# Low halves of woven weights: made by an adding DMA in place of GpSimd's subtraction, and used last

## The chip, the core and the metric

The kernel runs on one core of a Trainium2 chip. The metric is the device time of one execution in microseconds (us), lower is better. Engines: TensorE (PE, with its weight loads PEld), VectorE (DVE), ScalarE (ACT), GpSimd (POOL) and SyncE (SP, which issues nearly all DMAs).

## The reference

One layer of a hybrid model over 640 tokens: 128 of a prompt and 512 of a 2-D grid, with 1024 features. Everything is float32.

```python
def _trunk_layer(x, cvec, s0, ctx_k, ctx_v, p):
    sh1, sc1, g1, sh2, sc2, g2 = _modulation(cvec, p["w_ada"], p["b_ada"])
    h = _rmsnorm(x, p["norm1_g"]) * (1.0 + sc1) + sh1
    u_rw, u_na, gate_rw, gate_na = jnp.split(h @ p["w_in"], IN_SPLITS, axis=-1)
    o_rw, s_new = _rwkv_branch(u_rw, s0, ...)      # recurrent scans, forward and backward
    ...
    o_na = _na_latent(q, k, v, ctx_k, ctx_v, p["na_rpb"])   # or _na_context for the prompt
    merged = (jax.nn.sigmoid(gate_rw) * (o_rw @ p["w_o_rwkv"])
              + jax.nn.sigmoid(gate_na) * (o_na @ p["w_o_na"]))
    x = x + g1 * (merged @ p["w_out"])
    h2 = _rmsnorm(x, p["norm2_g"]) * (1.0 + sc2) + sh2
    x = x + g2 * ((jax.nn.silu(h2 @ p["ffn_w1"]) * (h2 @ p["ffn_w3"])) @ p["ffn_w2"])
    return x, s_new, k, v
```

## The kernel before, in words

**Split products.** A float32 matrix is written as the sum of a rounded matrix (`hi`, type float32r) and the remainder (`lo`). A product is three matmuls: hi weights by hi input, hi weights by lo input, lo weights by hi input. `feat_gen` (L188) yields these one at a time for one half of the tokens (320 of 640) and one chunk of 128 output features: 8 tiles of 128 input features by 3 products are 24 matmuls, two halves 48.

**Weight chunks.** `wdma` (L157) has SyncE load a chunk (128x1024 float32, 512 KB) into a staging tile `wst`, of which there are two in this stage. `wcast` (L166) has ScalarE copy it into `whi`, which rounds it (L170). Then VectorE or GpSimd writes `wlo` = `wst` - `whi` (L175); GpSimd does so in pieces of 256 columns. The next load into the same buffer starts when that subtraction has read it.

**Units.** Between about 120 and 690 us of the span the kernel works off 47 units (`stream`, L740) in an order written out by hand: `k`, `r`, `v`, `l` (projections of the recurrent branch), `g` (gates), then the merges `a0` to `a7` (neighbourhood output, 4 input tiles, chunks of 128x512, 24 matmuls) and `b0` to `b7` (recurrent output, 3 input tiles, 128x384, 18 matmuls; the order is `b2`, `b4`, `b3`, `b5`). A string with one letter for each unit says which engine makes its low half: VectorE for the first nine and `a4`, GpSimd (`p`) for the other 37: 22 chunks of 128x1024, 7 of 128x512 and 8 of 128x384. Units `k1` to `b7` are GpSimd's.

**The weave.** From about 254 us on, the units fill TensorE's time between the parts of the recurrent scan, in four passes over pairs of heads. Each pass has `main`, `inv` (inversion of triangular blocks on VectorE: `pr` at L1249 and `RL` at L1253, ending in `f`, L1262), `carry` (a chain that goes back and forth between TensorE and ScalarE, L1323, L1326, L1350) and `out` (L1411). `AG` (L1104) and `ZV` (L1375) are VectorE's inputs to such products. A table sets how many matmuls of a unit go between two steps. A unit's cast is issued an eighth of the way into the unit before it. Inside the weave the orders of TensorE, GpSimd, VectorE and ScalarE are those of the code; SyncE's queue, and the other engines after the weave, go by the scheduler's simulated times.

**Merges and the end.** Before `a0`, twelve loads (`o_load`, L1435) fetch the neighbourhood output's hi and lo parts (`o_d_80`, `o_d_81`) into two tiles `o`, which take the places of `h` (hi, lo). A merge unit multiplies `o`, and VectorE adds the gate (`mt`, L1463). After `b7` comes a product over the last input tile with one more chunk of `w_o` (L1575), whose sums are multiplied with gate parts `pre` and `tr` (loads at L1569), and then the product with `w_out`, added to the residual `x`.

Of the kernel before, what the change touches and what calls it, by code (L numbers as in the profile page):

```python
# [7 lines left out]
F32 = mybir.dt.float32  # L8
F32R = mybir.dt.float32r
AF = mybir.ActivationFunctionType  # L10
ALU = mybir.AluOpType
# [90 lines left out]
def V(ap, dims, off=0):  # L102

    return bass.AP(ap.tensor, ap.offset + off, [list(ap.ap[0])] + [list(d) for d in dims])
# [3 lines left out]
def body(ctx: ExitStack, tc: tile.TileContext, xs, xp, cols, consts, w_ada, b_row, w_rw, w_qkv,  # L108
# [3 lines left out]
    pe, act, dve, pool, sp = nc.tensor, nc.scalar, nc.vector, nc.gpsimd, nc.sync  # L112
# [22 lines left out]
    def nm(s):  # L135
        cn[0] += 1
        return f"{s}_{cn[0]}"
# [28 lines left out]
    def wcast(w, eng=None):  # L166
        st, n, pl, nhl = w
        hi = pl.tile([P, 1024], F32R, tag="whi", bufs=nhl, name=nm("whi"))
        lo = pl.tile([P, 1024], F32R, tag="wlo", bufs=nhl, name=nm("wlo"))
        act.copy(hi[:, :n], st[:, :n])  # L170
        eng = eng or dve
        step = 256 if eng is pool else n
        for a in range(0, n, step):
            b = min(a + step, n)
            eng.tensor_tensor(out=lo[:, a:b], in0=st[:, a:b], in1=hi[:, a:b].bitcast(F32), op=ALU.subtract)  # L175
        return hi, lo

    def wload(src, eng=None):
        return wcast(wdma(src), eng)
# [8 lines left out]
    def feat_gen(ps, chunk, act_hl, nk, t0, t1, width=128, wcol=0, k0=0):  # L188

        hi, lo = chunk  # L190
        xh, xl = act_hl
        n = 0
        for kt in range(nk):
            a = kt * width + wcol
            for (w, x) in ((hi, xh), (hi, xl), (lo, xh)):
                pe.matmul(ps[:, :t1 - t0], w[:, a:a + 128], x[:, k0 + kt, t0:t1],  # L196
                          start=n == 0, stop=n == 3 * nk - 1)
                n += 1
                yield

    def drain(g):
        for _ in g:
# [2 lines left out]
    def feat_mm(*args, **kw):  # L205
        for _ in feat_gen(*args, **kw):
            pass
# [295 lines left out]
    def proj_gen(ci, out, ps_, usb, utag, ubufs, w):  # L503
        U = usb.tile([P, 643], F32, tag=utag, bufs=ubufs, name=nm("U"))
        pool.memset(V(U[:, :], [[513, 2]]), 0.0)
        pool.memset(U[:, 642:643], 0.0)
        ps0 = ps_()
        yield from feat_gen(ps0, w, (hh, hl), 8, 0, H2)
        later(lambda: act.copy(U[:, 1:321], ps0[:, :H2]))
        ps1 = ps_()  # L510
        yield from feat_gen(ps1, w, (hh, hl), 8, H2, NT)

        def u_out():
            act.copy(U[:, 321:513], ps1[:, 0:192])
            act.copy(U[:, 514:642], ps1[:, 192:320])

        def shift(a, b, u):
            o = out[:, a:b]
            n = b - a
            act.activation(o, U[:, u:u + n], AF.Identity, scale=dcol(dm, ci))  # L520
            dve.scalar_tensor_tensor(out=o, in0=U[:, u - 1:u - 1 + n], scalar=col("mu0", ci),
                                     in1=o, op0=ALU.mult, op1=ALU.add)
            dve.scalar_tensor_tensor(out=o, in0=U[:, u + 1:u + 1 + n], scalar=col("mu1", ci),
                                     in1=o, op0=ALU.mult, op1=ALU.add)

        later(u_out, (0.6, 0))
        later(lambda: shift(512, 640, 514), (0.4, 0.7), 2)
        later(lambda: shift(0, 512, 1), (0.8, 1.5), 5)
# [190 lines left out]
    def unit(g, e):  # L719

        i, eng = int(g[1:]), eng_of(e)
        if g[0] in "ab":
            return 24 if g[0] == "a" else 18, lambda: merge_load(g[0], i), \
                lambda wt: merge_cast(*wt, eng), lambda w: merge_gen(g[0], i, w)
        if g[0] == "g":
            return 48, lambda: wdma(w_rw[15 + i]), lambda w: wcast(w, eng), \
                lambda w: gate_gen(i, w, flps, sb, gtag[-1])
        ci, dst = {"k": (4 + i, kt_), "r": (i, rt_), "v": (8 + i, vp0), "l": (12 + i, lg_)}[g[0]]
        return 48, lambda: wdma(w_rw[ci]), lambda w: wcast(w, eng), \
            lambda w: proj_gen(ci, dst, flps, sb, "U", len(gtag), w) if g[0] != "l" else lora_gen(i, w)  # L730
# [48 lines left out]
    with s1:  # L779
# [25 lines left out]
        with s1a:  # L805
            for b, dst, gcol in ((0, qT, dcol(dqg)), (1, kT, col("kg"))):
# [10 lines left out]
                for i in range(5):  # L817
# [10 lines left out]
                                      in0=V(qr[:, :], [[64, 8], [1, 64]]),  # L828
                                      in1=V(r[:, :], [[1, 8], [0, 64]]), op=ALU.mult)
                    if b == 1 and i == 4:  # L830
                        kout = tb.tile([P, 512], F32, tag="vt", bufs=2, name="kout")
                        dve.tensor_tensor(out=V(kout[:, :], [[64, 8], [1, 64]]),
                                          in0=V(qn[:, :], [[64, 8], [1, 64]]),
                                          in1=V(kgb[:, :], [[0, 8], [1, 64]]), op=ALU.mult)
# [4 lines left out]
                    for f in range(4):  # L839
                        src = pst[:, f * 128:(f + 1) * 128]  # L840
                        if i < 4:
                            out = V(dst[f], [[1, 2], [8, 64]], 2 * i)
                            src = V(src, [[64, 2], [1, 64]])
                        else:
                            out = dst[f][:, 512:640]
# [27 lines left out]
        with ExitStack() as s1b:  # L873
# [127 lines left out]
            with tc.manual_schedule(engines=FIRST):  # L1001
                for k, step in enumerate(PRM["na"].split()):
                    a, p, b, q, n = (int(x) for x in step.split("."))
# [994 lines left out]
```

## Time and profile before

| | |
|---|---|
| time, median of 3 runs | 1202.04 us (1201.33 to 1202.62) |
| profiled execution | 1203.88 us, of which the span is 1202.1 us |
| mean granted TensorE clock | 0.975 |
| busy: TensorE, weight loads, VectorE, ScalarE, GpSimd | 94%, 84%, 67%, 42%, 23% |
| GpSimd's subtractions (L175) | 118 pieces, 100.7 us |

A profile row with "x4" joins four instructions in a row; where a bracket ends the row, it gives the idle time of the engine ahead of it and what ended that. A row of waits gives the waiting engine and line, the engine and line that released it, the total in us, how often, and the longest. All times within an execution count from the start of the span.

### The profile page before, as it was taken

What the parts mean: (1) busy time and instruction counts of PE and PEld (TensorE: products, weight loads), DVE (VectorE), ACT (ScalarE), POOL (GpSimd) and SP (SyncE); (2) the same over time, 40 slices, a digit from 0 to 9 for tenths busy, and PEclk for the clock granted to TensorE, in tenths of its full rate; (3) what the DMA queues carried; (4) which work ended last, traced back from release to release, by engine and by line L of the source; (5) the groups of instructions that cost most, each with busy time, mean ns of one, the idle gap of its engine ahead of it and who ended that gap; (6) DMA issues with size and microseconds to landing.
All of it is one profiled execution on the core that took longest, in us unless ns stands there. A gap on an engine that the chain in (4) does not pass through costs nothing.

```text
span 1202.1 us, 26930 instructions
## 1 busy us (share of the span) xinstructions
PE 1134.1 (94%) x11160; PEld 1006.9 (84%) x11160; DVE 799.6 (67%) x1630; ACT 503.6 (42%) x1016; POOL 271.8 (23%) x354
## 2 busy tenths in 40 slices
PE   6999999999899899999879999989999999999998
PEld 4688877788888888888778878889889989998997
DVE  4565555569659848946584584888568756875675
ACT  4444655553454564355322331754224422442240
POOL 1162244343224324332221360200001000000000
PEclk8999999999899999999889989999999999999999
DMA  9762767531211221120442571312312231222222
GB/s 335 251 122 83 245 207 231 190 123 49 66 48 37 89 63 54 66 70 30 167 131 75 178 271 58 106 36 88 106 53 88 89 103 56 88 89 88 69 72 104
DMA packets 56578, 134.48 MB, mean 112 GB/s; under 512 B 7140, under 2 KB 22116, under 8 KB 56456
## 3 DMA queue, kind: packets, MB, share of 16 engines
q1 hardware_dynamic: 55592, 131.56, 33.6%
q8 instruction: 88, 1.44, 0.5%
q10 hardware_dynamic: 864, 1.20, 0.3%
q14 instruction: 34, 0.28, 0.1%
HBM read 118.41 MB, written 14.32 MB: 110 GB/s over the span
## 4 chain that ended last, share of the span: by engine, by line
PE 58%; DVE 15%; DMA 2%; ACT 2%; issue 2%; SPq 0%; POOL 0%; DVEq 0%; ACTq 0%
PE f L1717 21%; PE acc L283 16%; PE fl L196 10%; DVE pr L1249 2%; DVE RL L1253 2%; PE w L1363 1%; PE w L1323 1%; PE w L1350 1%; DVE AG L1156 1%; PE w L1335 1%; PE mm L196 1%; DVE TG L1159 1%; DVE Rt L1283 1%; DVE AG L1104 1%; DMA tr<-trw_d 1%
## 5 line engine op out<-in xcount | busy, mean ns | idle before, releaser
L196 PE MATMUL fl<-h,whi 128*128 128x320 f32 x704 | 169.7, 322 | 0.0
L175 POOL TENSOR_TENSOR wlo<-wst,whi 128x256 fp32r<-128x256 f32 x118 | 100.7, 882 | 203.2 <-ACT whi L170 199.8
L1717 PE MATMUL f<-t,whi 128*128 128x320 f32 x640 | 141.4, 309 | 0.0
L1717 PE MATMUL f<-b,whi 128*128 128x320 f32 x608 | 136.4, 312 | 3.6 <-ACT b L185 1.8
L283 PE MATMUL acc<-whi,u 128*128 128x512 f32 (+1 forms) x448 | 136.1, 385 | 0.0
L196 PEld LDWEIGHTS fl<-h,whi 128*128 128x128 f32 x704 | 120.6, 191 | 4.5 <-issue 0.2
L170 ACT CAST whi<-wst 128x1024 fp32r<-128x1024 f32 (+2 forms) x86 | 81.9, 957 | 79.3 <-PE acc L283 28.3
L196 PE MATMUL fl<-h,wlo 128*128 128x320 f32 x352 | 114.1, 324 | 0.0
L1717 PEld LDWEIGHTS f<-t,whi 128*128 128x128 f32 x640 | 107.0, 188 | 0.0
L1717 PEld LDWEIGHTS f<-b,whi 128*128 128x128 f32 x608 | 102.8, 190 | 4.8 <-ACT b L185 2.2
L1772 POOL TENSOR_TENSOR ws<-wst 128x512 f32<-128x512 f32 x20 | 27.8, 1390 | 341.6 <-DVE wlo L1761 226.7
L1717 PE MATMUL f<-t,wlo 128*128 128x320 f32 x320 | 98.9, 309 | 0.0
L283 PEld LDWEIGHTS acc<-whi,u 128*128 128x128 f32 x448 | 83.5, 188 | 16.7
L1717 PE MATMUL f<-b,wlo 128*128 128x320 f32 x304 | 94.7, 311 | 1.4 <-DVE wlo L1761 1.4
L1758 ACT CAST whi<-ws 128x1024 fp32r<-128x1024 f32 x40 | 42.0, 1050 | 108.7 <-PE f L1717 48.4
L283 PE MATMUL acc<-wlo,u 128*128 128x512 f32 (+1 forms) x224 | 86.3, 385 | 0.0
L175 DVE TENSOR_TENSOR wlo<-wst,whi 128x1024 fp32r<-128x1024 f32 (+1 forms) x49 | 60.6, 1243 | 35.3 <-ACT whi L170 34.8
L283 PE MATMUL acc<-whi,h 128*128 128x512 f32 x240 | 79.3, 404 | 0.2 <-DVE h L397 0.2
L196 PE MATMUL fl<-o,whi 128*128 128x320 f32 x224 | 58.9, 342 | 13.7 <-DVE mt L1463 5.7
L196 PEld LDWEIGHTS fl<-h,wlo 128*128 128x128 f32 x352 | 67.4, 192 | 2.6 <-issue 0.2
L1557 DVE SCALAR_TENSOR_TENSOR tt<-acc,G 128x512 f32<-128x512 f32 (+1 forms) x51 | 34.7, 680 | 50.7 <-PE acc L283 50.7
L196 PE MATMUL mm<-h,whi 128*128 128x320 f32 x288 | 67.8, 323 | 0.0
(332 smaller groups left out, 2587.6 us busy)
## 6 DMA issues: line engine op xcount, KB each, us to landing
wst<-in_w_dram SPq DMA_DIRECT2D x66, 512.0 KB
wst<-in_w_rw_dram SPq DMA_DIRECT2D x31, 512.0 KB
wa<-in_w_ada_dram SPq DMA_DIRECT2D x24, 512.0 KB
f<-in_w_ada_dram SPq DMA_DIRECT2D x16, 512.0 KB
wst<-in_w_qkv_dram SPq DMA_DIRECT2D x12, 512.0 KB
o<-o_d SPq DMA_DIRECT2D x14, 320.0 KB
x<-in_xs_dram SPq DMA_DIRECT2D x8, 512.0 KB
wa<-in_w_ada_dram SPq DMA_DIRECT2D x16, 256.0 KB
```

The source lines that it names most:

```text
L170: act.copy(hi[:, :n], st[:, :n])
L175: eng.tensor_tensor(out=lo[:, a:b], in0=st[:, a:b], in1=hi[:, a:b].bitcast(F32), op=ALU.subtract)
L196: pe.matmul(ps[:, :t1 - t0], w[:, a:a + 128], x[:, k0 + kt, t0:t1], start=n == 0, stop=n == 3 * nk - 1)
L283: pe.matmul(pss[i][:, a:b], lhs(x, kt, ts_), w[:, cs_], start=ki == 0 and n == 0, stop=ki == last and n == 2)
L1104: dve.tensor_tensor(out=AG[rr, c, h, :], in0=c64(S.kk[rr, :], d), in1=S.P65[d][rr, :, 0:64], op=ALU.mult)
L1156: dve.tensor_tensor(out=AG[oth, ls, h, :], in0=sq(pg, n)[oth], in1=V(K[oth, :], [[0, n], [1, 64]], KO["strict"]), op=ALU.mult)
L1249: dve.tensor_tensor(out=prv, in0=V(RL[:, s + 1 + a, :], [[32, b - a], [0, s]], s), in1=V(RL[:, s, :], [[0, b - a], [1, s]]), op=ALU.mult)
L1253: dve.tensor_tensor(out=dst, in0=dst, in1=prv, op=ALU.add)
L1557: dve.scalar_tensor_tensor(out=tt, in0=ps[:, a:b], scalar=c, in1=G[:, g, sl], op0=ALU.mult, op1=ALU.mult)
L1717: pe.matmul(ps[:, :H2], w_[:, c_], x_[:, kt, :], start=first and kt + n == 0, stop=last and kt == 3 and n == 2, skip_group_check=more)
L1758: act.copy(r[0][:, :width], src())
L1772: eng_x(PRM["se"][i - 1]).tensor_tensor(out=o_, in0=x, in1=y, op=op)
```

## The change

For a unit of GpSimd, ScalarE first writes the negated chunk, rounded, to `wlo`; then GpSimd issues one DMA that adds the staged chunk to `wlo` (`accum_op`), and ScalarE makes `whi` as before. The sum is `wst` minus the rounded `wst`, the same low half. VectorE's units keep their subtraction. In `feat_gen` the order of a half's matmuls is new for all units: all products with hi weights come first, then all with low weights.

```diff
@@ -167,12 +167,12 @@
         st, n, pl, nhl = w
         hi = pl.tile([P, 1024], F32R, tag="whi", bufs=nhl, name=nm("whi"))
         lo = pl.tile([P, 1024], F32R, tag="wlo", bufs=nhl, name=nm("wlo"))
+        if eng is pool:
+            act.activation(lo[:, :n], st[:, :n], AF.Copy, scale=-1.0)
+            pool.dma_start(lo[:, :n].bitcast(F32), st[:, :n], accum_op=ALU.add)
         act.copy(hi[:, :n], st[:, :n])
-        eng = eng or dve
-        step = 256 if eng is pool else n
-        for a in range(0, n, step):
-            b = min(a + step, n)
-            eng.tensor_tensor(out=lo[:, a:b], in0=st[:, a:b], in1=hi[:, a:b].bitcast(F32), op=ALU.subtract)
+        if eng is not pool:
+            dve.tensor_tensor(out=lo[:, :n], in0=st[:, :n], in1=hi[:, :n].bitcast(F32), op=ALU.subtract)
         return hi, lo
 
     def wload(src, eng=None):
@@ -190,13 +190,14 @@
         hi, lo = chunk
         xh, xl = act_hl
         n = 0
-        for kt in range(nk):
-            a = kt * width + wcol
-            for (w, x) in ((hi, xh), (hi, xl), (lo, xh)):
-                pe.matmul(ps[:, :t1 - t0], w[:, a:a + 128], x[:, k0 + kt, t0:t1],
-                          start=n == 0, stop=n == 3 * nk - 1)
-                n += 1
-                yield
+        for ps_ in (((hi, xh), (hi, xl)), ((lo, xh),)):
+            for kt in range(nk):
+                a = kt * width + wcol
+                for (w, x) in ps_:
+                    pe.matmul(ps[:, :t1 - t0], w[:, a:a + 128], x[:, k0 + kt, t0:t1],
+                              start=n == 0, stop=n == 3 * nk - 1)
+                    n += 1
+                    yield
 
     def drain(g):
         for _ in g:
```

Lines behind L170 move by one. ScalarE's queue at the first two GpSimd units (`wlo_2813` is `k1`'s; `U` and `on` are other work), before:

```order
L542 ACTIVATE U_2746<-mm_2747 128x320
L170 COPY whi_2812<-wst_2671 128x1024
L185 COPY on_2535<-po_2822 128x128
L542 ACTIVATE U_2801<-mm_2802 128x320
L170 COPY whi_2912<-wst_2799 128x1024
L542 ACTIVATE U_2845<-mm_2846 128x320
```

and with the change:

```order
L543 ACTIVATE U_2746<-mm_2747 128x320
L171 ACTIVATE wlo_2813<-wst_2671 128x1024
L173 COPY whi_2812<-wst_2671 128x1024
L185 COPY on_2535<-po_2820 128x128
L543 ACTIVATE U_2801<-mm_2802 128x320
L543 ACTIVATE U_2843<-mm_2844 128x320
L171 ACTIVATE wlo_2911<-wst_2799 128x1024
```

The negated copy (L171) stands right ahead of each cast, and nothing else is put between; the second unit's cast moves one place back among the `U` rows.

GpSimd's queue at the same place, before:

```order
L921 TENSOR_TENSOR L_2709<-L_2709,m_2710 128x128
L175 TENSOR_TENSOR wlo_2813<-wst_2671,whi_2812 128x256 x4
L1496 MEMSET Nt 128x1280
L505 MEMSET U_2901 128x2
L506 MEMSET U_2901 128x1
L175 TENSOR_TENSOR wlo_2913<-wst_2799,whi_2912 128x256 x4
L1203 MEMSET ZV 64x2x64 x2
```

and with the change:

```order
L922 TENSOR_TENSOR L_2709<-L_2709,m_2710 128x128
L172 DMA wlo_2813<-wst_2671 128x1024
L1497 MEMSET Nt 128x1280
L506 MEMSET U_2899 128x2
L507 MEMSET U_2899 128x1
L172 DMA wlo_2911<-wst_2799 128x1024
L1204 MEMSET ZV 64x2x64 x2
```

Each group of four subtractions becomes one DMA issue at the same place in the queue.

SyncE's queue at the loads of `o` ahead of the merges (`o_d_80` hi, `o_d_81` lo; `tna_d` is a store of gate parts), before:

```order
L543 DMA tna_d<-fl_7589 128x320
L1435 DMA o_7754<-o_d_81 128x640 x2
L1435 DMA o_7753<-o_d_80 128x640 x3
L1435 DMA o_7754<-o_d_81 128x640
L1435 DMA o_7753<-o_d_80 128x640
L1435 DMA o_7754<-o_d_81 128x640
L1435 DMA o_7753<-o_d_80 128x640
L1435 DMA o_7754<-o_d_81 128x640
L1435 DMA o_7753<-o_d_80 128x640
L1435 DMA o_7754<-o_d_81 128x640
L543 DMA tna_d<-fl_7640 128x320
```

and with the change:

```order
L163 DMA wst_7723<-in_w_o_dram 128x512
L544 DMA tna_d<-fl_7545 128x320
L1436 DMA o_7710<-o_d_81 128x640 x6
L1436 DMA o_7709<-o_d_80 128x640 x6
L544 DMA tna_d<-fl_7596 128x320
L163 DMA wst_7942<-in_w_o_dram 128x512
```

The loads of the two parts, which alternated from the third on, now come as six of the low part and then six of the high part.

SyncE's queue at the end of the merges, before:

```order
L1449 DMA mx_9051<-trw_d 128x640
L1569 DMA pre_9175<-trw_d 128x640
L163 DMA wst_9155<-in_w_out_dram 128x1024
L163 DMA wst_9527<-in_w_out_dram 128x1024
L163 DMA wst_9575<-in_w_out_dram 128x1024
L1547 DMA x_0_9131<-in_xs_dram 128x1024
L1547 DMA x_1_9132<-in_xs_dram 128x1024
L1547 DMA x_2_9133<-in_xs_dram 128x1024
L1547 DMA x_3_9134<-in_xs_dram 128x1024
L1547 DMA x_4_9135<-in_xp_dram 128x1024
L1569 DMA tr_9177<-trw_d 128x640
L1569 DMA tr_9179<-trw_d 128x640
```

and with the change:

```order
L163 DMA wst_9105<-in_w_o_dram 128x8x128
L1570 DMA pre_9131<-trw_d 128x640
L163 DMA wst_9111<-in_w_out_dram 128x1024
L163 DMA wst_9483<-in_w_out_dram 128x1024
L1548 DMA x_0_9087<-in_xs_dram 128x1024
L1548 DMA x_1_9088<-in_xs_dram 128x1024
L1548 DMA x_2_9089<-in_xs_dram 128x1024
L1548 DMA x_3_9090<-in_xs_dram 128x1024
L1548 DMA x_4_9091<-in_xp_dram 128x1024
L1570 DMA tr_9133<-trw_d 128x640
L1570 DMA tr_9135<-trw_d 128x640
```

One chunk of `w_out` that stood ahead of the loads of `x` and `tr` now stands behind them.

## The prediction

> **What bounds the kernel now.** I read the page first.
>
> ```profile
> span 1202.1 us, 26930 instructions
> PE 1134.1 (94%) x11160; PEld 1006.9 (84%) x11160; DVE 799.6 (67%) x1630; ACT 503.6 (42%) x1016; POOL 271.8 (23%) x354
> q1 hardware_dynamic: 55592, 131.56, 33.6%
> L175 POOL TENSOR_TENSOR wlo<-wst,whi 128x256 fp32r<-128x256 f32 x118 | 100.7, 882 | 203.2 <-ACT whi L170 199.8
> ```
>
> TensorE is busy for 94%, and GpSimd's subtraction (118 pieces, 100.7 us) lies beside it. The change can therefore win only where TensorE waits, and lose only where it makes TensorE wait anew. TensorE's waits in the stage that uses GpSimd's low halves (254 to 690 us), as engine, line, releaser, total, times, longest:
>
> ```profile
> PE w L1275 <- DVE f L1262: 6.6, 2, 5.8
> PE fl L196 <- DVE mt L1463: 5.7, 1, 5.7
> PE fl L196 <- DMA o<-o_d: 5.5, 2, 4.3
> PE w L1147 <- DVE out L1411: 4.2, 3, 2.0
> PE w L1125 <- DVE AG L1104: 2.6, 4, 1.0
> PE w L1323 <- DVE ZV L1375: 1.5, 1, 1.5
> ```
>
> TensorE never waits for a low half: no row names `wlo`. Five of the six rows end on VectorE, which is the bound in parts of this stage. The windows of the first inversion and of the matmuls behind it (span, then TensorE, weight loads, VectorE, ScalarE, GpSimd, granted clock, DMA share, GB/s):
>
> ```profile
> 267.00:305.00 38.00, 31.27 (x658) 29.78 (x660) 36.73 (x126) 14.06 (x32) 9.90 (x20) 0.97 0.16 52
> 304.40:314.00 9.60, 9.60 (x195) 9.26 (x195) 9.27 (x18) 3.79 (x9) 0.10 (x1) 0.74 0.22 74
> ```
>
> VectorE is busy for 36.73 of 38 us in the inversion, whose last result (`f`) TensorE waits 5.8 us for. Behind that wait the granted clock is 0.74, not 0.97: the wait is paid for twice.
>
> **What is removed: GpSimd's subtraction, and its hold on VectorE.** The timelines of VectorE and GpSimd in that inversion:
>
> ```profile
> 276.88 0.45 DVE L1253 TENSOR_TENSOR RL<-RL,pr 128x88 f32<-128x88 f32 x2
> 280.13 1.52 DVE L1253 TENSOR_TENSOR RL<-RL,pr 128x99 f32<-128x99 f32 x2
> ```
>
> ```profile
> 278.18 3.35 POOL L175 TENSOR_TENSOR wlo<-wst,whi 128x256 fp32r<-128x256 f32 x4 [8.22 <-ACT whi L170]
> 286.50 2.94 POOL L175 TENSOR_TENSOR wlo<-wst,whi 128x256 fp32r<-128x256 f32 x4 [4.90 <-ACT whi L170]
> 297.86 2.79 POOL L175 TENSOR_TENSOR wlo<-wst,whi 128x256 fp32r<-128x256 f32 x4 [8.41 <-ACT whi L170]
> ```
>
> The same pair of VectorE instructions, a few columns wider, takes 1.52 us beside GpSimd's subtraction and 0.45 without it. Three chunks cover 3.35 + 2.94 + 2.79 = 9.1 us of the inversion, so VectorE loses up to 9.1 x (1 - 0.45/1.52) = 6.4 us, ahead of a wait of 5.8. I take 5.3 (0.5 is left, since something still runs on GpSimd) and the clock behind it: 9.60 x (0.97 - 0.74)/0.97 = 2.3.
>
> The other waits on VectorE lie behind stages with fewer chunks in them or with other work. I take 0.6 of the other `f` wait (6.6 - 5.8), 1.5 of 2.6 for `AG`, 2.5 of 4.2 for `out`, 0.5 of 1.5 for `ZV` and only 1.0 of 5.7 for `mt` (the merge runs past the last inversion; its wait is VectorE's own queue). Bounds: nothing, and all of each. Gain: 5.3 + 2.3 + 0.6 + 1.5 + 2.5 + 0.5 + 1.0 = **13.7 us**.
>
> The Trainium skill (SBUF — State Buffer, section "Who interferes with whom") says that a `tensor_tensor` with both inputs in SBUF contends with GpSimd's reads, as the pair above does; by it the relief would be the whole 6.4 us.
>
> **What is added on ScalarE: a negated copy ahead of every cast** of a GpSimd unit. Groups of ScalarE (mean ns of one behind the busy time):
>
> ```profile
> L170 ACT CAST whi<-wst 128x1024 fp32r<-128x1024 f32 x24 | 25.0, 1041 | 6.1 <-PE mm L196 2.9 <-DMA wst<-in_w_o_dram 1.6 <-PE fl L196 1.5
> L170 ACT CAST whi<-wst 128x512 fp32r<-128x512 f32 x8 | 4.9, 617 | 15.4 <-PE fl L196 15.3
> L170 ACT CAST whi<-wst 128x384 fp32r<-128x384 f32 x8 | 4.1, 515 | 2.3 <-PE fl L196 2.2
> ```
>
> 22 units of 1.04, 7 of 0.62 and 8 of 0.52 make 31 us of ScalarE, which idles over half of the time, so most of it is hidden. It shows where a TensorE-to-ScalarE chain follows the cast at once. ScalarE's timeline at such places: a cast and the row behind it, and the rows behind three more casts, with the idle time between cast and row in brackets (none for `Rt`):
>
> ```profile
> 438.48 1.06 ACT L170 CAST whi<-wst 128x1024 fp32r<-128x1024 f32 x1
> 439.69 0.27 ACT L1326 COPY x<-w 128x128 f32<-128x128 f32 x1 [0.15 <-PE w L1323]
> ...
> 513.65 0.73 ACT L1294 COPY Rt<-w 32x320 f32<-32x320 f32 x2
> ...
> 524.91 0.37 ACT L1326 COPY x<-w 128x256 f32<-128x256 f32 x1 [0.43 <-PE w L1323]
> ...
> 547.13 0.27 ACT L1326 COPY x<-w 128x128 f32<-128x128 f32 x1 [0.29 <-PE w L1323]
> ```
>
> The delays are 1.04 less the idle time: 0.89 + 1.04 + 0.61 + 0.75 = **3.3 us** lost (0 to 8 if other places with some slack tip over).
>
> **What is added on the queues: the adding DMA.** No DMA of before is issued by GpSimd and none adds, so its price is bounded by rows. From the chain that ended last (start, us, transfer) and SyncE's timeline:
>
> ```profile
> 262.62 2.65 DMA ZV<-in_stt_dram
> 679.38 6.85 DMA wst<-in_w_o_dram
> ```
>
> ```profile
> 581.44 7.59 SPq L1435 DMA_DIRECT2D o<-o_d  x12
> ```
>
> A 32 KB load takes 2.65 us: my floor. q1 moves 131.56 MB in 33.6% of 16 x 1202.1 us, 20.4 GB/s per engine, so 512 KB take 1.6 us on 16 engines, and 3.2 if the add reads two sources at that rate. For the issue on GpSimd I take 1.0 us (SyncE's 7.59/12 = 0.63 below, the 2.8 of a removed chunk above). A full chunk lands 5.3 to 6.9 us after its negated copy, 256 KB after 4.45 to 5.25, 192 KB after 4.25 to 4.85; far above lies only the loaded 6.85 us.
>
> When is it needed? With low weights last, the first low matmul is the 17th of a full unit, the 9th of an `a` merge, the 7th of a `b` merge. ScalarE's casts and the TensorE rows that hold those positions:
>
> ```profile
> 252.99 1.04 ACT L170 CAST whi<-wst 128x1024 fp32r<-128x1024 f32 x1
> 671.18 0.51 ACT L170 CAST whi<-wst 128x384 fp32r<-128x384 f32 x1
> 681.93 0.51 ACT L170 CAST whi<-wst 128x384 fp32r<-128x384 f32 x1
> ```
>
> ```profile
> 262.26 0.46 PE L196 MATMUL fl<-h,whi 128*128 128x320 f32 x2
> 674.10 0.46 PE L196 MATMUL fl<-o,whi 128*128 128x320 f32 x2
> 686.99 0.46 PE L196 MATMUL fl<-o,whi 128*128 128x320 f32 x2
> ```
>
> The reordering alone costs nothing: the page counts one weight load for each matmul (x11160 both), in either order. The old cast's end is about when the negated copy ends. The tightest full unit (`k1`) then has 8.4 us, enough. Worked alike for the 15 merge units, `b3` has 2.4, `b7` 4.55, `b6` 4.5, `a5` 4.65, `a3`, `b5` and `b1` 5.0 to 5.1, the others 5.8 to 11.6. At the middle of the estimate `b3` comes 2.15 late and `a5` 0.2: **2.4 us** lost (0 to 4).
>
> A staging buffer now comes free when the add has landed (4.55 us behind the cast), not at GpSimd's end (1.15 us of work behind it):
>
> ```profile
> 678.21 1.15 POOL L175 TENSOR_TENSOR wlo<-wst,whi 128x256 fp32r<-128x256 f32 x2 [2.75 <-ACT whi L170]
> ```
>
> SyncE's loads queue behind that. It shows at the end: ScalarE's cast of the last chunk of `w_o` waits for its load already, and TensorE waits in the product with it (L1575).
>
> ```profile
> 686.33 1.05 ACT L170 CAST whi<-wst 128x1024 fp32r<-128x1024 f32 x1 [1.65 <-DMA wst<-in_w_o_dram]
> ```
>
> ```profile
> PE fl L1575 <- DVE tr L1576: 2.4, 1, 2.4
> ```
>
> The load of 679.38 starts some 4.55 - 1.2 = 3.3 later: **3.3 us** lost (0 if the late merges cover it). But the order puts the `tr` loads one weight chunk earlier on SyncE, worth **1.0** of those 2.4 us.
>
> Last, the twelve loads of `o`. They alternated in part; now all six low parts go first, so the first high part moves from 3rd to 7th place: 4 x 0.63 = 2.5 us. The low half of `h` comes free some eight matmuls earlier, which gives back part. TensorE waits there already (5.5 us), so I charge **2.0 us** (0 to 4.5).
>
> The sum: -13.7 + 3.3 + 2.4 + 3.3 - 1.0 + 2.0 = **-3.7 us**. The profiled execution took 1203.88 us, 1.84 above the median of 1202.04; I would expect 1200.2 for its like, and **1198.3 us** against the median.
>
> **The rivals.** *The low halves come late in the merges (slower).* The place is `a3` to `b7`; the price is the latency less each unit's allowance. At 6.5 us that is 4.1 (`b3`) + 2.0 (`b6`) + 1.95 (`b7`) + 1.85 (`a5`) + 4.4 (`a3`, `b5`, `b1`) + 0.7 (`b2`) = 15.0 instead of 2.4, so -3.7 - 2.4 + 15.0 = +8.9: 1210.9 us. At 8 us it is 29.2: 1225 us. The forecast's gain is gone from about 5.3 us, only 0.5 above my bound for 192 KB. For it: `wst` took 6.85 us in a busy stretch. Against: the DMA share was 0.16 and 0.22 in the windows above. The Trainium skill speaks for it (SBUF — State Buffer, section "SBUF: two separate sides"): a GpSimd DMA's descriptors cannot be written while VectorE holds the port the two share. No run here shows it yet.
>
> *VectorE gets no relief (slower).* If GpSimd's DMA work holds VectorE back as its subtraction did, the gain is 0 and the costs stay: +10.0, 1212.0 us. For it: VectorE's slow rows name no cause but what runs beside them. Against: a DMA need not read its 512 KB through GpSimd.
>
> *The relief goes through whole (faster).* All of the waits on VectorE vanish: 6.6 + 5.7 + 4.2 + 2.6 + 1.5 + 2.3 = 22.9 less 10.0, so 1189.1 us. Against: VectorE's order is unchanged, and its own chains stay.
>
> *It cancels.* Within 2.4 us of 1202.04, 0.2%, about what a measurement of this kernel tells from no change.
>
> **How the numbers follow.** Forecast (down by over 2.4 us, to about 1193) 0.35, whole relief 0.10, cancels 0.15, late low halves 0.22, no relief 0.18. Faster 0.45, same 0.15, slower 0.40. The range of 1188 to 1215 takes in the whole relief, the no-relief case and, for the merges, a latency of up to 7 us (19.5 us of stalls: 1215); beyond it lie slower DMAs and a larger gain. The forecast's own range is 1193 to 1199.6.
>
> **What would show it.** Right: VectorE's `RL` pairs near 0.45 us throughout the inversion, the wait for `f` under 1 us, 0.97 of clock behind it; waits on `wlo` only in `b3` and `a5`; the wait for `o` 1 to 3 us longer. Wrong: `wlo` waits in most merges, the adding DMA over 5.3 us after its copy, or `RL` pairs still at 1.5 us.

## The result, and the profile after

The changed kernel takes 1193.01 us (median of six runs, 1190.16 to 1195.39) against 1201.68 us of before beside it (1199.8 to 1204.12). The ratio is 0.9932, with a 95% interval of 0.9915 to 0.9949: 8 us faster. Forecast were 1198.3 us, a gain of 3.7 us. The profiled execution took 1191.72 us.

The page of the changed kernel, parts 1 and 3:

```profile
span 1189.7 us, 26921 instructions
PE 1124.1 (94%) x11160; PEld 998.3 (84%) x11160; DVE 777.5 (65%) x1630; ACT 530.5 (45%) x1053; POOL 205.1 (17%) x273
q1 hardware_dynamic: 55592, 131.56, 33.6%
q0 software_dynamic: 5328, 14.94, 6.8%
```

GpSimd's busy time fell by 67 us and ScalarE's rose by 27. VectorE's fell by 22 us, although VectorE executes the same 1630 instructions. The adding DMAs are a new queue, q0.

TensorE's waits in the same stage as before (254 to 690 us; the product behind the merges, L1576, now begins inside it):

```profile
PE fl L197 <- DMA o<-o_d: 10.0, 1, 10.0
PE fl L197 <- DVE mt L1464: 4.7, 1, 4.7
PE fl L1576 <- ACT o L185: 3.1, 1, 3.1
PE fl L197 <- DMA wlo<-wst: 2.1, 2, 1.4
PE fl L197 <- DVE P L1464: 2.1, 2, 1.5
PE w L1148 <- DVE out L1412: 2.0, 1, 2.0
...
PE w L1324 <- DVE ZV L1376: 1.5, 1, 1.5
```

The waits for `f` (6.6 us) and `AG` (2.6) are gone, that for `out` halved, that for `mt` fell by 1.0 us and that for `ZV` stayed. The wait for `o` nearly doubled. Low halves are waited for twice, 2.1 us.

The windows of the first inversion and of what follows:

```profile
267.00:305.00 38.00, 37.24 (x768) 35.73 (x761) 37.37 (x141) 19.12 (x39) 3.54 (x12) 1.00 0.44 113
304.40:314.00 9.60, 9.19 (x140) 8.04 (x140) 2.88 (x9) 5.74 (x14) 3.94 (x4) 1.00 0.45 103
```

TensorE is busy for 37.24 us of the inversion's window where it was 31.27, and the granted clock behind it is 1.00 where it was 0.74. GpSimd's and VectorE's timelines show why:

```profile
277.69 0.86 POOL L172 DMA_DIRECT2D wlo<-wst  x1 [10.11 <-ACT wlo L171]
```

```profile
277.40 0.44 DVE L1254 TENSOR_TENSOR RL<-RL,pr 128x100 f32<-128x100 f32 x2
278.13 0.45 DVE L1254 TENSOR_TENSOR RL<-RL,pr 128x110 f32<-128x110 f32 x2
278.87 0.46 DVE L1254 TENSOR_TENSOR RL<-RL,pr 128x108 f32<-128x108 f32 x2
```

GpSimd spends 0.86 us on the issue, and the `RL` pairs around it stay at 0.44 to 0.46 us, where a pair beside the subtraction had taken 1.52. Over the whole inversion VectorE's 96 operations `pr` and `RL` alone, before and then with the change (span, VectorE, clock, DMA share, GB/s):

```profile
267.00:305.00 38.00, 23.27 (x96) 0.97 0.16 52
267.00:305.00 38.00, 16.74 (x96) 1.00 0.44 113
```

The same 96 operations take 6.5 us less.

**Where the time went.** For every run I took from TensorE's timeline the start of the first matmul of each unit. The table gives, for stretches between such starts, the kernel's time less that of before (us, one profiled execution each; the last column ends with the last matmul of the kernel). What lies ahead of `k1` is left out: starts of `k1` range from 256.1 to 261.8 us, also among kernels with equal instructions there. Executions of one kernel differ by several us (31 of before took 1195.93 to 1205.93), and the profiled one need not be typical: inv0_dma's took 1188.03 us, the shortest of its eight, against a median of 1194.08. So a difference of 1 or 2 us in a long stretch is not secure.

| kernel | k1 to g4 | g4 to g5 | g5 to g14 | g14 to a1 | a1 to b3 | b3 to b7 | b7 to end | k1 to end |
|---|---|---|---|---|---|---|---|---|
| length before | 34.98 | 17.64 | 258.58 | 28.89 | 73.07 | 12.28 | 512.87 | 938.31 |
| changed | +0.71 | -7.56 | -9.04 | +5.45 | -2.32 | +2.17 | +0.39 | -10.20 |
| reorder_only | -0.08 | +0.16 | +0.67 | +0.05 | -0.24 | -0.53 | -0.73 | -0.70 |
| dma_only | +1.42 | -7.55 | -5.61 | +2.93 | -0.23 | +5.19 | -0.75 | -4.60 |
| neg_only | -0.08 | -4.30 | +1.32 | +1.12 | +0.27 | -0.05 | +0.48 | -1.24 |
| inv0_dma | +0.05 | -7.55 | -2.78 | -0.57 | +0.02 | -0.52 | -1.30 | -12.65 |
| o_fix | +0.48 | -7.56 | -9.01 | +4.27 | -1.73 | +2.96 | +0.05 | -10.54 |
| bsub | +0.70 | -7.56 | -9.48 | +5.46 | -2.26 | -0.46 | -0.37 | -13.97 |
| full_dma | +0.70 | -7.56 | -7.58 | -0.43 | +0.02 | +0.45 | -0.94 | -15.34 |
| no_add | +0.12 | -7.55 | -8.04 | +1.44 | -0.85 | -0.86 | -1.52 | -17.26 |
| a0_sub | +0.41 | -7.56 | -9.13 | +5.54 | -2.35 | +2.00 | +0.89 | -10.20 |
| best | +0.42 | -7.55 | -9.32 | +3.98 | -0.15 | +0.14 | +1.49 | -10.99 |
| a1_sub | +0.43 | -7.56 | -8.62 | +2.60 | -2.06 | +2.43 | -0.86 | -13.64 |
| best_a1 | +0.43 | -7.56 | -9.43 | -0.60 | -1.96 | -0.44 | -0.86 | -20.42 |

The row of the changed kernel is the whole account from `k1` on: 7.56 us won at the first inversion and 9.0 in the later passes, 5.5 lost at the loads of `o`, 2.3 won behind them, and 2.2 lost in the last merges.

Three of these stretches, from `g4`, `g5` and `g14` on, each before and then with the change (columns as in the windows above):

```profile
295.04:312.68 17.64, 11.82 (x211) 11.24 (x209) 17.30 (x49) 5.30 (x12) 2.79 (x4) 0.81 0.12 40
293.44:303.52 10.08, 10.08 (x210) 9.56 (x209) 9.79 (x16) 6.24 (x13) 0.85 (x1) 1.00 0.50 135
...
312.68:571.26 258.58, 244.17 (x4073) 219.13 (x4072) 176.20 (x433) 130.40 (x319) 87.74 (x122) 0.98 0.18 58
303.52:553.06 249.54, 240.57 (x4074) 216.40 (x4072) 162.98 (x434) 146.00 (x336) 40.35 (x71) 0.99 0.37 96
...
571.26:600.15 28.89, 23.41 (x385) 21.12 (x384) 14.70 (x56) 9.56 (x21) 8.39 (x12) 0.88 0.50 173
553.06:587.40 34.34, 24.30 (x385) 21.68 (x384) 14.34 (x56) 10.50 (x23) 6.89 (x10) 0.80 0.51 161
```

TensorE's matmuls in a stretch are the same in both kernels. Its length less TensorE's busy time is waiting; where the busy time itself changes, the granted clock changes with it. At the first inversion 5.82 us of waiting and 1.74 of busy time went. From `g5` to `g14` it is 5.4 of waiting and 3.6 of busy time. At the loads of `o` 4.6 us of waiting and 0.9 of busy time were added.

### The profile page after: what moved, and what is told of

Read it like the earlier page. It is cut to its first block, busy times and chain, and to the rows that moved or that the text cites. A ratio compares the mean times of both kernels' runs of the same rounds, so it can differ in the third digit from the quotient of the medians.

```text
span 1189.7 us, 26921 instructions
## 1 busy us (share of the span) xinstructions
PE 1124.1 (94%) x11160; PEld 998.3 (84%) x11160; DVE 777.5 (65%) x1630; ACT 530.5 (45%) x1053; POOL 205.1 (17%) x273
## 3 DMA queue, kind: packets, MB, share of 16 engines
q0 software_dynamic: 5328, 14.94, 6.8%
q8 instruction: 88, 1.44, 0.5%
## 4 chain that ended last, share of the span: by engine, by line
PE 65%; DVE 8%; ACT 3%; DMA 2%; issue 1%; SPq 0%; ACTq 0%; DVEq 0%; POOLq 0%
PE f L1718 23%; PE acc L284 17%; PE fl L197 13%; DMA wlo<-wst 1%; DVE pr L1250 1%; PE w L1324 1%; PE w L1351 1%; DVE RL L1254 1%; PE mm L197 1%; PE w L1364 1%; PE w L1336 1%; PE w L1148 1%; DMA o<-o_d 1%; PE w L1196 1%; PE w L1126 1%
## 5 line engine op out<-in xcount | busy, mean ns | idle before, releaser
L197 PE MATMUL fl<-h,whi 128*128 128x320 f32 x704 | 126.5, 319 | 0.8 <-issue 0.8
L197 PEld LDWEIGHTS fl<-h,whi 128*128 128x128 f32 x704 | 106.1, 188 | 5.6 <-issue 0.9
L172 POOL DMA_DIRECT2D wlo<-wst x37 | 32.6, 881 | 232.4 <-ACT wlo L171 212.9
L197 PE MATMUL fl<-h,wlo 128*128 128x320 f32 x352 | 66.5, 321 | 0.0
L197 PE MATMUL fl<-o,whi 128*128 128x320 f32 x224 | 46.3, 337 | 16.8 <-DMA o<-o_d 10.0
L1759 ACT CAST whi<-wst 128x1024 fp32r<-128x1024 f32 (+1 forms) x48 | 41.3, 869 | 42.3 <-PE acc L284 37.6
L1718 PEld LDWEIGHTS f<-t,wlo 128*128 128x128 f32 x320 | 60.1, 188 | 0.0
```

The costliest lines, as they stand in the source:

```text
L172: pool.dma_start(lo[:, :n].bitcast(F32), st[:, :n], accum_op=ALU.add)
L1718: pe.matmul(ps[:, :H2], w_[:, c_], x_[:, kt, :], start=first and kt + n == 0, stop=last and kt == 3 and n == 2, skip_group_check=more)
L1759: act.copy(r[0][:, :width], src())
```

## The experiments

### Which part of the change brings the gain

**reorder_only**: before with the new `feat_gen`, and GpSimd's subtraction.

```diff
-        for kt in range(nk):
-            a = kt * width + wcol
-            for (w, x) in ((hi, xh), (hi, xl), (lo, xh)):
+        for ps_ in (((hi, xh), (hi, xl)), ((lo, xh),)):
+            for kt in range(nk):
+                a = kt * width + wcol
+                for (w, x) in ps_:
```

> Before, with the new order of matmuls in a half (low weights last) and GpSimd's subtraction kept. Theory A (the gain is VectorE's relief from GpSimd's subtraction): no gain; 0 to +4 us against before, all of it at the loads of o, whose wait grows from 5.5 towards 10 us because the low part of h comes free first. Theory B (the gain comes from the order of matmuls, since TensorE needs each low half later): 6 us or more faster than before.

Measured: 1201.92 against 1200.16 us, ratio 1.0005 (0.9984 to 1.0025). Theory B falls. The order alone neither gains nor costs, not even at `o`, whose loads in this kernel still alternate in part. The waits stand as they did:

```profile
PE w L1276 <- DVE f L1263: 5.8, 1, 5.8
PE fl L197 <- DMA o<-o_d: 5.8, 1, 5.8
```

**dma_only**: the changed kernel with that edit of `feat_gen` undone (lines with + and - above change places).

> The changed kernel with the old order of matmuls (hi, hi, low for each tile). Theory A: all of VectorE's relief stays (about -16 us up to the last gate unit), the wait for o goes back to about 5 us (worth 5 against the changed kernel), and the low halves are late in a5, b3, b5 and b6 (about 6 us instead of 2): 8 to 13 us faster than before. Theory B: no gain, 1200 us or above.

Measured: 1196.05 against 1200.16 us, ratio 0.9958 (0.9941 to 0.9974). The whole 7.55 us at the first inversion stay and 5.6 of the 9.0 behind it. Low halves are late more often:

```profile
PE fl L196 <- DMA wlo<-wst: 7.9, 6, 2.8
```

These are six waits of 7.9 us together, against two of 2.1; between `b3` and `b7` 5.19 us are lost instead of 2.17. So the new order brings nothing by itself, but it pays for part of the DMA's latency. The gain was half of the least expected. The longest wait for `o` went to 5.6 us as expected, yet the time from `g14` to `a1` was still 2.9 us longer than before: the first sign that not only the order of these loads costs. (0.9 us of it are waits; the rest is TensorE's busy time, at a granted clock of 0.84 against 0.88.)

**neg_only**: before, with the negated copy added and its result overwritten.

```diff
+        if eng is pool:
+            act.activation(lo[:, :n], st[:, :n], AF.Copy, scale=-1.0)
         act.copy(hi[:, :n], st[:, :n])
```

> Before, with ScalarE's negated copy added ahead of each GpSimd unit's cast (GpSimd's subtraction then writes over it). The prediction's term: +3.3 us against before (0 to 8). Rival: ScalarE has room everywhere, within 1 us of before.

Measured: 1201.42 against 1200.16 us, ratio 0.9996 (0.9976 to 1.0017). In sum nothing, but the trace shows two things of opposite sign. From `g5` to `a1` the kernel loses 1.3 + 1.1 us; of the 1.1, 1.0 is not waiting but TensorE's busy time, at a lower granted clock (0.83 against 0.88). At the first inversion it gains 4.30 us, which neither theory had. Counted from the units' starts, GpSimd's subtractions begin about 1 us later there, behind the added copy. The second of them, and VectorE beside it:

```profile
285.04 6.72 POOL L177 TENSOR_TENSOR wlo<-wst,whi 128x256 fp32r<-128x256 f32 x4 [2.90 <-ACT whi L173]
```

```profile
286.93 0.45 DVE L1255 TENSOR_TENSOR RL<-RL,pr 128x114 f32<-128x114 f32 x2
287.31 0.44 DVE L1251 TENSOR_TENSOR pr<-RL 128x100 f32<-128x100 f32 x2
...
288.75 0.96 DVE L1251 TENSOR_TENSOR pr<-RL 128x88 f32<-128x88 f32 x2
```

Here GpSimd is the one that is held up: four pieces take 6.72 us instead of 2.94, while VectorE's pairs run on at 0.45 us, until some get slower again at 288.75. The wait for `f` fell to 1.7 us. VectorE's 96 operations of the inversion took 19.07 us, between the 23.27 of before and the 16.74 of the change. So the two engines do hold each other up. Which of them paid changed here together with a shift of about a microsecond; no run varies that shift by itself.

**inv0_dma**: before, with the copy and the DMA for the units `r1`, `g4`, `g5` alone (letter `m` in the string of engines; lines of `wcast`, and the string's first 15 letters):

```diff
-    wl="dddddddddpppppp...
+    wl="dddddddddppmmmp...
...
+        if dma:
+            act.activation(lo[:, :n], st[:, :n], AF.Copy, scale=-1.0)
+            pool.dma_start(lo[:, :n].bitcast(F32), st[:, :n], accum_op=ALU.add)
...
-        for a in range(0, n, step):
+        for a in range(0, n if not dma else 0, step):
```

> Before, with only the three units whose low halves are made during the first inversion (r1, g4, g5) changed to the negated copy and the adding DMA; matmuls in the old order. Theory A, by the prediction's terms for this place: the wait for f behind the inversion falls from 5.8 to about 0.5 us and the clock behind it stays near 0.97, so 5.3 + 2.3 = 7.6 us faster up to unit g5, and about as much at the end. Rival (GpSimd's work for the DMA holds VectorE as its subtraction did): within 1 us of before.

Measured: 1194.08 against 1200.16 us, ratio 0.9934 (0.9905 to 0.9962). Three of the 37 chunks bring what all of them bring. Between `g4` and `g5` it is 7.55 us, as in every kernel here that uses the DMA there. The wait of 5.8 us for `f` is gone (the later one, 0.8, stays), and VectorE's 96 operations take 16.71 us. It gains 2.8 us more up to `g14`, where nothing of it is changed: 2.0 are the two waits for `Rt` of before, which are gone here too, and 0.8 is TensorE's busy time. Why they go is not shown.

**no_add**: the changed kernel without its DMA.

```diff
-            pool.dma_start(lo[:, :n].bitcast(F32), st[:, :n], accum_op=ALU.add)
```

> The changed kernel with the adding DMA left out: the low halves of GpSimd's units stay the negated rounded weights, so the output differs; ScalarE's copies and the order stay. It tells what the DMA itself costs VectorE and TensorE. Theory A (its issue on GpSimd and its 15 MB hold nothing): within 1.5 us of the changed kernel up to g14, and 2 to 3 us faster behind b3. Rival (the DMA still holds VectorE in part): 3 us or more faster up to g14, with less of VectorE's time lost.

Measured: 1186.38 against 1199.4 us, ratio 0.9891 (0.9868 to 0.9914). Up to `g14` it is at 0.12 - 7.55 - 8.04 = -15.5 us, the changed kernel at -15.9, and VectorE's 96 operations take 16.72 us against 16.74: the adding DMA takes nothing from VectorE there. It costs behind `g14`: 5.45 against 1.44 us up to `a1`, and 2.17 against -0.86 from `b3` to `b7`.

### What the gain is lost to

The rows of the changed kernel around `a0`, from the timelines of SyncE, GpSimd and TensorE, and the DMA issues of GpSimd at 564 to 567 us (size, us from issue to landing):

```profile
562.20 8.15 SPq L1436 DMA_DIRECT2D o<-o_d  x12
```

```profile
565.23 0.92 POOL L172 DMA_DIRECT2D wlo<-wst  x1 [5.22 <-ACT wlo L171]
```

```profile
573.93 3.07 PE L197 MATMUL fl<-o,whi 128*128 128x320 f32 x7 [10.04 <-DMA o<-o_d]
```

```profile
wlo<-wst POOLq DMA_DIRECT2D x1, 256.0 KB, 8.5
```

**o_fix**: the changed kernel, with `feat_gen` in the old order for `g14` alone.

```diff
-        for ps_ in (((hi, xh), (hi, xl)), ((lo, xh),)):
+        for ps_ in (((hi, xh), (hi, xl)), ((lo, xh),)) if late else (((hi, xh), (hi, xl), (lo, xh)),):
...
-            yield from feat_gen(ps, w, (hh, hl), 8, a, b)
+            yield from feat_gen(ps, w, (hh, hl), 8, a, b, late=i != 14)
```

> The changed kernel, with the old order of matmuls in the one unit ahead of the merges (g14), so that both parts of h come free together and the loads of o alternate again. Theory A (the order of these loads cost the change some 5 us): the wait for o falls from 10.0 to about 5.5 us, 4 to 6 us faster than the changed kernel at the end of the merges. Rival: the adding DMA of a0 shares the engines with the twelve loads and is late in either order, so the time lost moves into a0: within 1.5 us of the changed kernel at unit a1.

Measured: 1192.04 against 1199.4 us, ratio 0.9937 (0.9912 to 0.9962), as the changed kernel. TensorE's first wait for `o` fell as forecast, but `a0` then stops three times more:

```profile
571.67 0.90 PE L197 MATMUL fl<-o,whi 128*128 128x320 f32 x2 [3.99 <-DMA o<-o_d]
...
574.30 1.64 PE L197 MATMUL fl<-o,whi 128*128 128x320 f32 x3 [1.72 <-DMA o<-o_d]
...
576.89 0.64 PE L197 MATMUL fl<-o,whi 128*128 128x320 f32 x1 [0.95 <-DMA o<-o_d]
```

From `g14` to `a1` 4.27 us are lost instead of 5.45 (1.95 of waiting and 2.31 of busy time, at a granted clock of 0.79). Theory A falls for this term, and the rival had the time right.

**bsub**: the changed kernel with GpSimd's subtraction for `b3`, `b5`, `b6`, `b7` (from here on `m` stands for the DMA and `p` for the subtraction; the letters of `a0` to `b7`):

```diff
-mmmmdmmmmmmmmmmm
+mmmmdmmmmmmmpppp
```

> The changed kernel, with GpSimd's subtraction again for the four last merges b3, b5, b6, b7. If the low halves that come late there cost what the trace shows (2.2 us between b3 and b7), the time between these units falls by about 2.2 us, and the product behind them starts 2 to 3 us earlier. Rival: VectorE is held back again there and gives it back: no difference.

Measured: 1189.11 against 1199.4 us, ratio 0.9911 (0.9888 to 0.9934). The stretch from `b3` to `b7` goes from +2.17 to -0.46, and no other stretch by over 0.8 us: that loss was the late low halves.

**full_dma**: the DMA for the 22 full units only; all merges by GpSimd's subtraction, and the old order of matmuls in them and in `g14`.

```diff
-mmmmdmmmmmmmmmmm
+ppppdppppppppppp
```

> The adding DMA for the 22 full units only, GpSimd's subtraction for all merges, old order of matmuls in g14 and the merges. By theory A it keeps all of the relief up to g14 (about 16 us), pays the old 5.5 us for o and nothing for late low halves: 4 to 8 us faster than the changed kernel, about 0.985 to 0.988 of before. Rival (the merges' own subtractions hold VectorE and eat it): as the changed kernel.

Measured: 1185.6 against 1199.4 us, ratio 0.9887 (0.9865 to 0.991). No loss is left from `g14` on (-0.43, +0.02, +0.45): the merges' adding DMAs, with the new order around them, cause it. The 2.3 us between `a1` and `b3` are not won either: TensorE's wait for `mt` stands at 5.7 us as before, against 4.7 in the changed kernel.

**a0_sub**: the changed kernel with GpSimd's subtraction for `a0`. **best**: the same and for `b3`, `b5`, `b6`, `b7`, with the old order in these and in `g14`.

```diff
-mmmmdmmmmmmmmmmm
+pmmmdmmmmmmmmmmm  (a0_sub)
+pmmmdmmmmmmmpppp  (best)
```

> The changed kernel with GpSimd's subtraction for the one merge a0, whose adding DMA runs among the twelve loads of o; orders of matmuls and loads as changed. Theory C (the 5.5 us lost between g14 and a1 are mostly the adding DMA of a0 on the engines that load o, and only some 1.4 us their order): the loss between g14 and a1 falls to 1 to 2 us, 3 to 5 us faster than the changed kernel at a1. Rival (it is the order of the loads): the loss stays near 5 us.

> The adding DMA for the full units and for a1 to a3, a5 to a7, b0, b1, b2, b4; GpSimd's subtraction for a0, b3, b5, b6, b7; old order of matmuls in g14 and in those five. Theory C: no loss between g14 and a1 (as with the DMA for full units alone, -0.4 us), 2.3 us of VectorE's relief between a1 and a5 as in the changed kernel, nothing late at the end: about 19 us faster than before from unit k1 to the end, 6 us faster than the changed kernel and 2 faster than with the DMA for full units alone (which is at the edge of what five rounds tell). Rival: the relief between a1 and a5 was only the give-back of the late a0, then it equals the kernel with the DMA for full units alone.

Measured: 1193.34 against 1202.28 us, ratio 0.9929 (0.9907 to 0.995), and 1188.18, ratio 0.9885 (0.9864 to 0.9906). From `g14` to `a1` +5.54 and +3.98: my theory C failed as I had put it. The adding DMA at 565.46 us was still there in `best`, landing after 8.9 us:

```profile
wlo<-wst POOLq DMA_DIRECT2D x1, 256.0 KB, 8.9
```

It was that of `a1`, whose cast comes before `a0` has begun; `a0`'s had landed before the loads. The next two runs use this.

**a1_sub**: the changed kernel with GpSimd's subtraction for `a1` alone. **best_a1**: as `best`, with GpSimd's subtraction for `a1` in the place of `a0`'s, and the old order in both.

```diff
-mmmmdmmmmmmmmmmm
+mpmmdmmmmmmmmmmm  (a1_sub)
+mpmmdmmmmmmmpppp  (best_a1)
```

> Theory C named the wrong unit: the adding DMA among the twelve loads of o is a1's (issued 2 to 3 us behind the first of them, it lands after 8.5 to 9.1 us where others take 3 to 5), not a0's. The changed kernel with GpSimd's subtraction for a1 alone: the loss between g14 and a1 falls from 5.5 to 1 to 2 us (the kernel without any adding DMA lost 1.4). Rival (the order of the loads alone): the loss stays at 5.5 us.

> The adding DMA for the full units and a0, a2, a3, a5 to a7, b0, b1, b2, b4; GpSimd's subtraction for a1, b3, b5, b6, b7; old order of matmuls in g14 and in a0, a1 and those four. If a1's DMA was the cause: within 1 us of no loss between g14 and a1, and 16 to 18 us faster from unit k1 to the end than before; 0.986 to 0.988 of before in time. Rival: as the kernel before this one, 11 us from k1 to the end.

Measured: 1188.82 against 1200.45 us, ratio 0.9905 (0.9874 to 0.9937), and **1183.18** us, ratio **0.9852** (0.9821 to 0.9883). With one chunk made otherwise the loss from `g14` to `a1` falls from 5.45 to 2.60 us, a little above the 1 to 2 expected. What is left is the order of matmuls and with it of the loads, since the old order in `g14`, `a0` and `a1` takes it to -0.60 in best_a1, where TensorE waits once:

```profile
569.87 0.90 PE L200 MATMUL fl<-o,whi 128*128 128x320 f32 x2 [5.08 <-DMA o<-o_d]
```

This is the fastest kernel here, 1.5% under before, and a little faster than expected (20.42 us from `k1` to the end in its profiled execution, 16 to 18 expected).

## Why the prediction was right in direction, and where its size was off

- **The first inversion: right.** Forecast were 5.3 us of waiting and 2.3 of clock, 7.6 together; 7.56 were measured, and inv0_dma shows that the three chunks named do it alone. The mechanism was right too: VectorE was to be relieved of up to 6.4 us and was relieved of 6.5. The parts were 5.82 of waiting and 1.74 of clock, so that the sum fits to 0.1 us is luck.
- **The later passes: under-sized, and the clock left out.** Of the terms that fall between `g5` and `g14` I credited 5.1 us and charged 3.3 for ScalarE, 1.8 net; 9.04 were won. Of these 3.6 are busy time of TensorE at a higher granted clock (0.99 against 0.98), a term that I had counted behind the first inversion only. In the trace of before the clock is 0.50 for three stretches of 3.4 us there (from 353.8, 463.1 and 497.2 us), with the change for one (from 345.3). The other 5.4 are waits. Of `AG`'s wait 2.6 us went (1.5 forecast), of `out`'s 2.2 (2.5), of `f`'s 0.8 (0.6), of `ZV`'s none (0.5). Two waits for `Rt` of 2.0 us, in a row I had not quoted, are gone too, but they also go in inv0_dma, which changes nothing in these passes. How much of the clock's part follows from the waits that went is open: the wait of 2.0 us for `out` that is left with the change is not followed by a lower clock.
- **ScalarE's copies: the size was right, most places were not.** TensorE's waits for ScalarE in the rows of `w` (254 to 690 us) sum to 2.5 us before, to 5.7 in neg_only, which adds the copies alone, and to 5.4 with the change. That is 3.2 and 2.9 us more, against 3.3 forecast. But at `x` (L1326), where I had put 2.25, only 0.8 came; the largest row is another, here before, in neg_only and with the change:

```profile
PE w L1078 <- ACT pre L1073: 0.9, 3, 0.4
...
PE w L1080 <- ACT pre L1075: 2.3, 3, 1.3
...
PE w L1079 <- ACT pre L1074: 1.9, 3, 1.3
```

- **Loads of `o`: under-sized, and half the cause missed.** I charged 2.0 us (0 to 4.5) for their order; 5.45 were lost. Two causes share them, and their costs do not add. With the new order of the loads and `a1`'s adding DMA 5.45 to 5.54 us are lost (changed, bsub, a0_sub). With the new order and no such DMA 1.44 to 2.60 are lost (no_add, a1_sub). With the old order and that DMA it is 2.93 to 4.27 (dma_only, best, o_fix), and with neither nothing (full_dma, best_a1). I looked only at when the DMA's result is needed, not at whom its bytes delay.
- **Behind `a1`: right for the wait.** The 2.32 us won up to `b3` are not the loss at `o` coming back: best_a1 loses nothing at `o` and wins 1.96 there. The wait for `mt` fell by 1.0 us, as forecast. The rest is TensorE's busy time (65.15 us before, 63.93 with the change, at a granted clock of 0.95 and 0.98).
- **Late low halves: right.** 2.4 forecast, 2.17 measured, in the last merges. The places were partly others, so the sum is right partly by luck: `b3` waits 0.71 us (2.15 forecast), and `b6` 1.36 where `a5` was expected:

```profile
659.90 0.71 PE L197 MATMUL fl<-o,wlo 128*128 128x320 f32 x3 [0.71 <-DMA wlo<-wst]
...
670.20 0.70 PE L197 MATMUL fl<-o,wlo 128*128 128x320 f32 x3 [1.36 <-DMA wlo<-wst]
```

- **The end of the merges: not told from nothing.** 3.3 - 1.0 = 2.3 us forecast, 0.39 measured from `b7` to the end, a column that runs from -1.52 to +1.49 among these kernels. The parts did move as forecast. SyncE issued the load of the last chunk of `w_o` 6.1 us ahead of the start of `b7` before and 2.4 ahead with the change, 3.7 later (3.3 forecast). In the product behind it TensorE's wait for `tr` fell from 2.4 to 0.6 us (1.0 forecast), and that for ScalarE's `o` grew from 1.5 to 3.1. That the later load makes this wait longer is not shown. The rows for `o` before and for `tr` with the change:

```profile
PE fl L1575 <- ACT o L185: 1.5, 1, 1.5
...
PE fl L1576 <- DVE tr L1577: 0.6, 1, 0.6
```

- **The DMA's price: about right.** Issue 0.86 us (1.0 taken), and from issue to landing, by size:

```profile
wlo<-wst POOLq DMA_DIRECT2D x22, 512.0 KB, 4.5
wlo<-wst POOLq DMA_DIRECT2D x7, 256.0 KB, 3.8
wlo<-wst POOLq DMA_DIRECT2D x8, 192.0 KB, 3.9
```

  My bounds (5.3 to 6.9, 4.45 to 5.25, 4.25 to 4.85, counted from the copy's end) lay above these medians; single ones in traffic lay beyond them.
- **The rivals.** "No relief" is refuted by no_add and inv0_dma. "Late in the merges" came at the forecast's own size (2.17 us), not at the rival's 15. The measured time lies between the forecast and "whole relief".

Stretch by stretch, forecast and measured: -7.6 and -7.56 at the first inversion, -1.8 and -9.04 up to `g14`, +2.0 and +5.45 at `o`, -1.0 and -2.32 up to `b3`, +2.4 and +2.17 in the last merges, +2.3 and +0.39 at the end. So the direction came from the mechanism that was named, and the largest miss is that of the later passes, 7.2 us, of which the loss at `o` took back 3.5.

## What to carry to other kernels

Moving an elementwise operation off GpSimd is worth what it takes from VectorE in the stretches where TensorE waits for VectorE; here the three chunks of the first inversion gave alone what all 37 gave net of their costs (ratios 0.9934 and 0.9932). Waits came together with a lower granted clock in several places here, so ask for that price at each wait that a change removes or makes longer, not at the longest alone. Before a step becomes a DMA, ask of each instance not only when its result is due but which loads run at that moment, and keep the old way for those few. An order of matmuls also decides which operand buffer comes free first, and through that the order of the next loads.

## What the runs showed of the hardware

- GpSimd's subtraction and VectorE's small two-input operations hold each other up, and either can be the loser. Before, four pieces took 2.94 us, with VectorE's pairs beside them at up to 1.54 us. In neg_only the first of the four took 4.55 us with the pairs at 0.43 to 0.46 for most of it; beside the other three the pairs took up to 1.52.
- The adding DMA moves 14.94 MB in 6.8% of 16 x 1189.7 us, 11.5 GB/s per engine; q1 moved 20.6 in the same execution. The Trainium skill (Collectives: The Full Stack, section "The bandwidth ceiling: the fold count and why AG ≠ RS ≠ AR") says of the add in a reduction that it needs two source reads, where a copy needs one. The ratio here is 0.56, near the half that this would give, but the two queues move different transfers and no run separates the cause.
- 256 KB landed 8.5 to 9.2 us after their issue among twelve loads of 320 KB (six kernels), against a median of 3.8; every other adding DMA landed within 6.8 us. And the granted clock falls to 0.50 in the wait for these loads. With the change it stays there for 13.7 us (567.1 to 580.8), before for 6.8 (586.0 to 592.8). The row from 568 to 571 us:

```profile
568.00:571.00 3.00, 0.00 (x0) 0.00 (x0) 0.00 (x0) 0.00 (x0) 0.00 (x0) 0.50 0.95 295
```

- The Trainium skill (SBUF — State Buffer, section "SBUF: two separate sides") warns that GpSimd cannot write the descriptors of a DMA that it issues while VectorE runs an operation in a 2-port performance mode. No run here shows such a delay. VectorE was busy for 37.37 of 38 us in the first inversion, and GpSimd's issues there took 0.85 to 0.86 us, like elsewhere (0.85 to 1.05 in all 37). The three DMAs landed after 6.2, 5.9 and 4.4 us there, but after 5.2, 4.5 and 4.4 in inv0_dma, where VectorE was as busy; what makes the difference is open. Which mode VectorE's operations ran in, no trace here shows.
